# Hybrid encoder layer: a fourth product pair in the gate-up stage, weight sums by an accumulating transfer, and eight gated tiles kept in HBM

## The chip, the core and the metric

The kernel runs on one core of a Trainium2 chip. The metric is the device time of one execution in microseconds (us). The core has a TensorE (PE) for matrix products, a VectorE (DVE), a ScalarE (ACT), a GpSimd (POOL) and a SyncE (SP), which work at the same time and wait for each other through semaphores. Each takes its own instructions strictly in the order in which they stand. Sixteen DMA engines move data between HBM and the on-chip memory (SBUF). SP issues nearly all transfers here, through a queue that is served in hardware; GpSimd can issue transfers too, and it prepares their descriptors in software. TensorE accumulates into the banks of PSUM.

## What is computed

One encoder layer on 256 tokens of width 2048, in float32: a feed-forward block (FFN), a mixing block, and a second FFN, each with a norm before and after it. The change touches the two FFNs alone.

```python
D_MODEL, SEQ, D_FF = 2048, 256, 5632

def rms_norm(x, gain):
    return x * lax.rsqrt(jnp.mean(x * x, axis=-1, keepdims=True) + EPS) * gain

def swiglu(x, w_gate_up, w_down):              # w_gate_up: 2048 x 11264, w_down: 5632 x 2048
    gate, up = jnp.split(x @ w_gate_up, 2, axis=-1)
    return (jax.nn.silu(gate) * up) @ w_down

x = x + 0.5 * rms_norm(swiglu(rms_norm(x, pre1), w1_gate_up, w1_down), post1)
h = rms_norm(x, pre_m); p = h @ W_in
x = x + rms_norm(concat(hgrn2(p), attention(p)) @ W_out, post_m)
x = x + 0.5 * rms_norm(swiglu(rms_norm(x, pre2), w2_gate_up, w2_down), post2)
```

## The kernel before, in words

**A product in three.** A float32 value is split into a high part `h` (a copy by ScalarE that rounds to the type TensorE multiplies, L176) and a low part `l` (the rest, a subtraction on VectorE, L177). A product of two such values is three matmuls: high by high, high by low, low by high (`three`, L435; the matmul is L441). Nearly all of TensorE's time is L441.

**The gate-up stage** of an FFN (`ffn`, L894) runs over 11 groups `g` (0 to 10) of 512 gate columns and 512 up columns. In each group it goes through eight pairs `u` (0 to 7): a pair is two blocks of 128 rows of the weights, 256 rows by 1024 columns, 1 MB, loaded by two transfers of 512 KB into a tile `raw` (L152; a pool `rawp` of three such tiles). The columns of `raw` are four blocks of 512: `b11`, `b12` (first 128 rows, gate and up), `b21`, `b22`. The split of a pair goes in halves of 1024 columns into tiles of two pools of five (`hip` for `h`, `lop` for `l`), so ScalarE and VectorE can be at most five halves ahead of TensorE.

**Plain and mixed pairs.** A plain pair is 8 products, 24 matmuls, from two split halves. A mixed pair (`seven`, L463) takes one of Winograd's forms of Strassen's scheme: it sees the pair as a 2x2 matrix of blocks and uses seven products, 21 matmuls, of sums of blocks. The sums of the activations are made once per FFN (`sums_in`, L934, kept as tiles `xs`). The sums of the weights are made each time, in place in `raw`:

```python
split_act(h, l, b11)                                         # one block of 512
four[:, 0:2] = four[:, 0::3] + four[:, 1:2]                  # L473: b11 + b12, b22 + b12
lower = split_half(raw, 1)                                   # b21, b22
b22 = b11 + b22                                              # L477
upper = split_half(raw, 0)
b21 = b22 + b21                                              # L479
last = split_half(raw, 1)
```

So a mixed pair costs three matmuls less than a plain one, and on VectorE an L473, an L477, an L479, a half block of 512 and a third half of 1024 more. The pairs 2, 4 and 6 are mixed from group 2 on, 2 and 4 in group 1, none in group 0. The four partial sums of the seven products are folded into the group's banks (`fold`, L507) near the end of a group: eight additions on VectorE (L516 to L539).

**After a group** `units` (L954) applies silu and the product of gate and up (L959, L960), turns the result on TensorE (L971, eight transposes) and splits it into two tiles `ht` of 512 KB, 22 in all, which are the left sides of the down stage. They lie in two pools, `late` (8) and `early` (14), until the down stage has used them.

**The down stage** (`Pairs`, L586) runs twice over the 22 pairs of the down weights (1024 output columns each), plain and mixed pairs in turn, in an order that is written out by hand (`orders`, L1009). It uses the same `raw`, `hip` and `lop`.

**Order.** The places of the instructions on each engine come from a scheduler that works before the run, with its own estimates; only a few stretches are fixed by hand. On the chip the order on each engine, SP and POOL among them, is fixed, and a late instruction holds back all that stand behind it.

## Time and profile before

| | |
|---|---|
| median of 3 runs | 1836.19 us (1835.5 to 1836.25) |
| span of the profiled execution | 1835.7 us |
| PE busy | 1821.5 us, 99% |
| DVE busy | 1620.7 us, 88% |
| ACT busy | 1099.7 us, 60% |
| POOL busy | 23.3 us, 1% |
| moved by DMA | 365.77 MB, 199 GB/s on the mean |
| POOL's own transfers | 0.14 MB |

The profile gives no time of the profiled execution beside its span, and the span lies within the three runs. A line such as L441 is one of the kernel before. "Busy" is the time in which an engine worked on something; a matmul's end is modelled, so the pace of TensorE is read from the distance between the starts of its matmuls, not from their durations. In a timeline a row is a start, a duration, the engine, the line, the operation and a count of equal instructions, with the idle time before the first of them and what ended it in brackets. A table of windows gives, for each stretch of the span, the busy time of each engine, the clock that was granted to TensorE, the busy share of the 16 DMA engines, and the rate in GB/s.

### The profile page before, as it was taken

The numbers are of one execution on the slowest core, as the hardware profiler recorded it, in microseconds if no ns is written. First come the engines' busy times: TensorE is split into PE (matmuls) and PEld (weight loads), VectorE is DVE, ScalarE is ACT, GpSimd is POOL, SyncE is SP. The second block draws the span as 40 slices with busy tenths as digits, with TensorE's granted clock in tenths as the row PEclk, the third lists the DMA queues.
The fourth block names the chain that finished last, engine by engine and source line by source line (L and its number), as shares of the span: only waits on it lengthen the run. The fifth ranks groups of instructions, "written<-read, shape, count | busy, mean of one in ns | idle before, by whom it ended". The sixth has DMA issues, their size and how long they took to land.

```text
span 1835.7 us, 22980 instructions
## 1 busy us (share of the span) xinstructions
PE 1821.5 (99%) x8492; PEld 1516.5 (83%) x8492; DVE 1620.7 (88%) x2047; ACT 1099.7 (60%) x1454; POOL 23.3 (1%) x39
## 2 busy tenths in 40 slices
PE   9999999999999999999999999999999999999998
PEld 7888888888888888888888888888888888888786
DVE  7989999999999998477787798989999999999897
ACT  7555555555666567476587556455556555566563
POOL 1000000000000001000000000000000000000000
PEclk9999999999999999999999999999999999999999
DMA  7555555556555576555454456555555555545564
GB/s 255 206 178 213 207 200 191 184 188 215 205 208 216 195 260 212 199 182 174 163 170 150 167 210 224 190 195 190 213 193 192 213 212 195 205 187 206 201 229 177
DMA packets 174737, 365.77 MB, mean 199 GB/s; under 512 B 9256, under 2 KB 44160, under 8 KB 173856
## 3 DMA queue, kind: packets, MB, share of 16 engines
q1 hardware_dynamic: 174272, 364.17, 56.0%
q8 instruction: 66, 1.08, 0.2%
q14 instruction: 47, 0.39, 0.1%
q0 software_dynamic: 352, 0.14, 0.0%
HBM read 360.06 MB, written 4.21 MB: 198 GB/s over the span
## 4 chain that ended last, share of the span: by engine, by line
PE 94%; ACT 2%; DVE 2%; DMA 1%; issue 0%; POOL 0%; DVEq 0%; SPq 0%; ACTq 0%; POOLq 0%
PE pa L441 40%; PE pb L441 36%; PE pa L309 5%; PE pa L314 3%; PE pa L364 2%; PE pa L362 2%; PE pa L363 2%; DMA raw<-in_w_ffn_down_dram 1%; DVE l L177 1%; ACT h L176 1%; PE pb L971 1%; PE pa L971 1%; PE pb L1376 0%; PE pb L1350 0%; PE pb L1454 0%
## 5 line engine op out<-in xcount | busy, mean ns | idle before, releaser
L176 ACT CAST h<-raw 128x1024 fp32r<-128x1024 f32 (+1 forms) x825 | 821.5, 1021 | 538.2 <-PE pb L441 146.9
L177 DVE TENSOR_TENSOR l<-raw,h 128x1024 fp32r<-128x1024 f32 (+1 forms) x825 | 950.1, 1180 | 135.7 <-ACT h L176 106.0
L441 PE MATMUL pa<-h,xt 128*128 128x512 f32 x1176 | 409.5, 390 | 0.1
L441 PE MATMUL pb<-h,xt 128*128 128x512 f32 x1060 | 376.9, 392 | 0.0
L441 PEld LDWEIGHTS pa<-h,xt 128*128 128x128 f32 x1176 | 220.8, 188 | 46.1 <-DVE xt L232 0.6
L441 PEld LDWEIGHTS pb<-h,xt 128*128 128x128 f32 x1060 | 199.0, 188 | 41.6 <-DVE pb L537 0.6
L441 PE MATMUL pa<-l,xt 128*128 128x512 f32 x588 | 229.2, 390 | 0.0
L441 PE MATMUL pb<-l,xt 128*128 128x512 f32 x530 | 206.4, 389 | 0.0
L441 PE MATMUL pb<-h,ht 128*128 128x512 f32 x464 | 163.5, 390 | 0.0
L441 PE MATMUL pa<-h,ht 128*128 128x512 f32 x464 | 162.7, 389 | 0.0
L441 PEld LDWEIGHTS pa<-l,xt 128*128 128x128 f32 x588 | 110.4, 188 | 23.4 <-DVE l L177 0.8
L473 DVE TENSOR_TENSOR raw<-raw 128x1024 f32<-128x1024 f32 x102 | 124.3, 1219 | 1.1
L309 PE MATMUL pa<-xt,h 128*128 128x512 f32 x512 | 124.4, 393 | 0.2 <-ACT h L176 0.2
L441 PEld LDWEIGHTS pb<-l,xt 128*128 128x128 f32 x530 | 99.6, 188 | 19.6
L309 PEld LDWEIGHTS pa<-xt,h 128*128 128x128 f32 x512 | 93.8, 188 | 18.6 <-ACT h L176 0.6
L441 PEld LDWEIGHTS pa<-h,ht 128*128 128x128 f32 x464 | 87.1, 188 | 18.1
L441 PEld LDWEIGHTS pb<-h,ht 128*128 128x128 f32 x464 | 87.1, 188 | 18.0
L441 PE MATMUL pb<-l,ht 128*128 128x512 f32 x232 | 90.3, 389 | 0.0
L441 PE MATMUL pa<-l,ht 128*128 128x512 f32 x232 | 90.3, 389 | 0.0
L441 PE MATMUL pa<-h,xs 128*128 128x512 f32 x232 | 80.8, 389 | 0.0
L441 PE MATMUL pb<-h,xs 128*128 128x512 f32 x232 | 80.8, 389 | 0.0
L479 DVE TENSOR_TENSOR raw<-raw 128x512 f32<-128x512 f32 x102 | 70.1, 688 | 1.8
(281 smaller groups left out, 2360.6 us busy)
## 6 DMA issues: line engine op xcount, KB each, us to landing
raw<-in_w_ffn_gate_up_dram SPq DMA_DIRECT2D x350, 512.0 KB, 4.7
raw<-in_w_ffn_down_dram SPq DMA_DIRECT2D x88, 1024.0 KB, 5.0
raw<-in_w_mix_in_dram SPq DMA_DIRECT2D x52, 1024.0 KB, 4.9
raw<-in_w_mix_out_dram SPq DMA_DIRECT2D x16, 1024.0 KB, 4.9
pg<-in_post_norm_ffn_dram SPq DMA_DIRECT2D x4, 512.0 KB, 7.4
X<-in_x_dram SPq DMA_DIRECT2D x2, 1024.0 KB, 8.4
bias<-row SPq DMA_DIRECT2D x16, 128.0 KB, 5.0
kept<-X SPq DMA_DIRECT2D x2, 1024.0 KB, 4.1
```

Of the source, the lines that this page charges most:

```text
L176: nc.scalar.copy(hi, src)
L177: nc.vector.tensor_tensor(lo, src, hi.bitcast(F32), ALU.subtract)
L309: nc.tensor.matmul(slot[f], weights(hs, kk, f), xcol(xt, k), start=(k == 0), stop=(k == KT - 1))
L314: nc.tensor.matmul(slot[f][:, 0:T], weights(ls, kk, f), xcol(xt, kh * 8 + kk, 0), start=False, stop=False,)
L362: nc.tensor.matmul(dst, xh, h[:, o : o + n], start=(k == 0), stop=False)
L363: nc.tensor.matmul(dst, xh, l[:, o : o + n], start=False, stop=False)
L364: nc.tensor.matmul(dst, xl, h[:, o : o + n], start=False, stop=(k == KT - 1))
L441: nc.tensor.matmul(self.bank(at), lhs, rhs, start=(n == 1), stop=n in (ends, self.of[at]), skip_group_check=n > ends,)
L473: nc.vector.tensor_tensor(four[:, 0:2], four[:, 0::3], four[:, 1:2].to_broadcast([P, 2, 512]), ALU.add)
L479: nc.vector.tensor_tensor(b21, b22, b21, ALU.add)
L971: nc.tensor.transpose(bank[:, o : o + P], zs[m][:, k * P : (k + 1) * P], ident)
```

## The change

In both FFNs the pairs 2, 3, 4 and 6 are mixed from group 2 on, and 2 and 3 in group 1. L473 is no longer done by VectorE: after each pair, `prepare` loads the mixed pair that is the third from there (two pairs lie between), splits its `b11` into tiles of their own (`h1`, `l1`, three each), and then has GpSimd read `b12` and `b22` from HBM once more and add them to `b11` and `b12` in SBUF during the transfer. The `raw` tiles of the pairs 2, 3 and 6 come from a new pool of two (`gated.room`), that of pair 4 from `rawp`. The room for that is made by keeping the first eight `ht` tiles in HBM: they are stored in the groups 1 to 4, two after pair 4 of each, and fetched again at the start of the down stage into the place of the new pool. The first order of the down stage is changed so that those eight come after seven others.

```diff
-    def load(src, between=None):
-        raw = rawp.tile([P, 2048], F32, tag="raw", name=nm("raw"))
+    def load(src, between=None, pool=rawp, **kw):
+        raw = pool.tile([P, 2048], F32, tag="raw", name=nm("raw"), **kw)
...
         def seven(self, u, aside=None):
 
-            raw = load(self.source(u))
+            ready = self.prepared.pop(u, None)
+            raw = ready[0] if ready else load(self.source(u))
...
-            h, l = self.one_block()
-            split_act(h, l, b11)
-
-            nc.vector.tensor_tensor(
-                four[:, 0:2], four[:, 0::3], four[:, 1:2].to_broadcast([P, 2, 512]), ALU.add
-            )
+            if ready:
+                h, l = ready[1:]
+            else:
+                h, l = self.one_block()
+                split_act(h, l, b11)
+
+                nc.vector.tensor_tensor(
+                    four[:, 0:2], four[:, 0::3], four[:, 1:2].to_broadcast([P, 2, 512]), ALU.add
+                )
             lower = split_half(raw, 1)
...
-    MIXED_IN = (2, 4, 6)
+    MIXED_IN = (2, 3, 4, 6)
+    LEAD = 3
+    AWAY = 8
...
+        def prepare(self):
+
+            at, g = self.pos + LEAD - 1, self.g
+            if at >= KT // 2:
+                at, g = at - KT // 2, g + 1
+            if g >= NG or (at not in self.mixed if g == self.g else at not in self.sums):
+                return
+            src = self.source(at, g)
+            raw = load(src, pool=rawp if at == MIXED_IN[2] else self.room, bufs=3 if at == MIXED_IN[2] else 2)
+            h, l = (self.room.tile([P, 512], F32R, tag=t, name=nm(t), bufs=3) for t in ("h1", "l1"))
+            split_act(h, l, raw[:, 0:512])
+            nc.gpsimd.dma_start(
+                raw[:, 0:1024].rearrange("p (k c) -> p k c", k=2), src[:, :, 1], accum_op=ALU.add
+            )
+            self.prepared[at] = raw, h, l
...
-            early_cm = tc.tile_pool(name=nm("he"), bufs=NU - LATE, reuse_waits="tile")
+            early_cm = tc.tile_pool(name=nm("he"), bufs=NU - LATE - AWAY, reuse_waits="tile")
             early = early_cm.__enter__()
-            hts, sums = [], {}
+            room_cm = tc.tile_pool(name=nm("gx"), bufs=1, reuse_waits="tile")
+            gated.room = room_cm.__enter__()
+            hts, sums, away = [], {}, {}
...
+            def put_away(u):
+                away[u] = dram.tile([P, 1024], F32, tag=f"ht{u}", name=nm("away"))
+                nc.sync.dma_start(away[u], hts[u].bitcast(F32).rearrange("p k i t -> p (k i t)"))
+
+            def fetch(u):
+                hts[u] = back.tile([P, 2, 2, T], F32R, tag="ht", name=nm("ht"))
+                nc.sync.dma_start(hts[u].bitcast(F32).rearrange("p k i t -> p (k i t)"), away[u])
...
-                    pool = early if g < NU - LATE else late
+                    pool = early if AWAY <= g < NU - LATE else late
...
-                    if g == 1 and u == 5:
-                        sums_in(MIXED_IN[2])
+                    if g == 1 and u in (5, 6):
+                        sums_in(MIXED_IN[u - 3])
+                    if u == 4 and 0 < g <= AWAY // 2:
+                        put_away(2 * g - 2)
+                        put_away(2 * g - 1)
+                    gated.prepare()
                 waiting = units(gated.c, rest if g else rs2)
                 next(waiting)
+            room_cm.__exit__(None, None, None)
             close_far()
+            back_cm = tc.tile_pool(name=nm("hb"), bufs=AWAY, reuse_waits="tile")
+            back = back_cm.__enter__()
             orders = [
-                [1, 3, 0, 5, 2, 7, 4, 9, 6, 11, 8, 13, 10, 15, 12, 14, 17, 16, 19, 18, 20, 21],
+                [9, 11, 8, 13, 10, 15, 12, 1, 14, 3, 0, 5, 2, 7, 4, 6, 17, 16, 19, 18, 20, 21],
...
             rows.work(2, lambda: next(waiting))
+            for i, u in enumerate((1, 3, 0, 5, 2, 7, 4, 6)):
+                fetch(u)
+                rows.work(3 + i // 2)
```

More of the change, by code (lines that the diff above doesn't have):

```diff
@@ L411, in __init__ @@
             self.tiles, self.sums = tiles, sums
+            self.prepared = {}
         def begin(self, order, c=None):
@@ L860, in group, with source @@
             self.begin(range(KT // 2), c)
-        def source(self, u):
-            return self.w[:, 2 * u : 2 * u + 2, :, self.g * 512 : (self.g + 1) * 512]
+        def source(self, u, g=None):
+            g = self.g if g is None else g
+            return self.w[:, 2 * u : 2 * u + 2, :, g * 512 : (g + 1) * 512]
         def left_sums(self, u):
             return self.sums[u]
+        def prepare(self):
[12 more added lines that the diff above has]
+            self.prepared[at] = raw, h, l
         def see(self, xt):
@@ L938, in sums_in @@
                 ws = sums_of(whole, room_for("s").rearrange("p (j t) -> p j t", j=4))
-                w = work.tile([P, 4, 2, P], F32R, tag="sp", name=nm("xs"), bufs=3)
+                apart = u == MIXED_IN[1]
+                w = (gated.room if apart else work).tile(
+                    [P, 4, 2, P], F32R, tag="sp", name=nm("xs"), bufs=1 if apart else 3
+                )
                 split_act(w[:, :, 0, :], w[:, :, 1, :], ws)
                 gated.sums[u] = w
+            def put_away(u):
[4 more added lines that the diff above has]
+                nc.sync.dma_start(hts[u].bitcast(F32).rearrange("p k i t -> p (k i t)"), away[u])
             def folded():
@@ L1024, in ffn @@
             rows.work(NU - 4)
+            back_cm.__exit__(None, None, None)
             early_cm.__exit__(None, None, None)
```

## The prediction, written before the changed kernel ran

> **What bounds the kernel now.** I read the page first (busy shares, the chain of waits), then the chain in order of time through the gate-up stage, then windows of one gate-up group each, then VectorE's timeline and waits within one group, then single transfers.
>
> ```profile
> span 1835.7 us, 22980 instructions
> PE 94%; ACT 2%; DVE 2%; DMA 1%; issue 0%; POOL 0%; DVEq 0%; SPq 0%; ACTq 0%; POOLq 0%
> 112.22 2.72 PE pa L441 x12
> 154.60 2.72 PE pa L441 x12
> 196.97 2.72 PE pa L441 x12
> 154.60:196.97 42.37, 42.37 (x192) 35.19 (x192) 39.41 (x47) 24.42 (x28) 0.00 (x0) 1.00 0.56 199
> 196.97:239.34 42.37, 42.37 (x193) 35.18 (x192) 39.41 (x47) 24.42 (x28) 0.00 (x0) 1.00 0.56 199
> 234.89 0.27 PE L971 MATMUL pa<-ident,z 128*128 128x128 f32 x1
> 235.00 0.27 PE L971 MATMUL pa<-ident,s 128*128 128x128 f32 x1
> ```
>
> The chain is TensorE. The same place of the gate-up loop returns every 42.37 us, and a run of 12 matmuls takes 2.72, so 0.2267 each; a group with three mixed and five plain pairs has 3x21 + 5x24 = 183 of them, 41.48 us, and eight transposes at 0.11 (from start to start) make 42.36. TensorE has no idle time there, at full clock. But the same windows show VectorE busy for 39.41 of 42.37. Its waits in the second window:
>
> ```profile
> DVE l L177 <- ACT h L176: 2.4, 2, 1.2
> DVE ht L177 <- ACT ht L176: 0.2, 1, 0.2
> 198.22 5.23 DVE L177 TENSOR_TENSOR l<-raw,h 128x1024 fp32r<-128x1024 f32 x5 [1.17 <-ACT h L176]
> 203.37 1.22 DVE L473 TENSOR_TENSOR raw<-raw 128x1024 f32<-128x1024 f32 x1
> 204.62 0.69 DVE L477 TENSOR_TENSOR raw<-raw 128x512 f32<-128x512 f32 x1
> 205.35 0.69 DVE L479 TENSOR_TENSOR raw<-raw 128x512 f32<-128x512 f32 x1
> 205.96 5.37 DVE L177 TENSOR_TENSOR l<-raw,h 128x1024 fp32r<-128x1024 f32 x5
> 217.53 4.63 DVE L177 TENSOR_TENSOR l<-raw,h 128x1024 fp32r<-128x1024 f32 x4 [1.19 <-ACT h L176]
> 224.42 1.21 DVE L177 TENSOR_TENSOR l<-raw,h 128x1024 fp32r<-128x1024 f32 x1
> 225.55 0.68 DVE L516 TENSOR_TENSOR z<-pb,s 128x512 f32<-128x512 f32 x1
> ```
>
> VectorE's idle time of a group is two waits of 1.17 and 1.19: after L479 it must wait until ScalarE has copied the half just summed (1.05) before it can subtract. That is a dependency inside VectorE's own work, not a wait for TensorE. So work, 42.37 - 2.6 = 39.8, and these waits fill the period: **VectorE is a second chain as long as TensorE's**, and a shorter TensorE alone buys little.
>
> **What the change takes from TensorE.** Nine groups of each FFN (2 to 10) get a fourth mixed pair: three matmuls of 0.2267 less, 18 x 0.68 = 12.2 us in all, 41.68 a group. The built program has 54 matmuls less, and GpSimd has 76 new transfers, 38 per FFN, so the change does what it says.
>
> **VectorE's work per group.** Away go three L473 of 1.25 at most (203.37 to 204.62): -3.6 at 1.2. The fourth mixed pair adds an L177 of 1024 columns (1.13, from 224.42 to 225.55) and an L177 of 512, an L477 and an L479 (0.61 to 0.73 from start to start; 2.0 together). 39.8 - 3.6 + 1.1 + 2.0 = 39.3. The waits after L479 become 1.2 at pair 6, and 0.5 at pairs 3 and 4, where the built order puts an `l1` of 0.6 in between; at pair 2 small work fills it: 2.2. Sum 41.5, just under TensorE's 41.68.
>
> **The new loads.** The two tiles of the new pool hold three pairs in turn (2, 3, 6, 2, ...), and a load waits for the last subtraction of the pair two places before. VectorE's built order around two of these, in the middle of the stage (tile 468 is pair 2, 482 pair 3, 514 pair 6, 495 pair 4, 541 pair 2 of the next group):
>
> ```
> L177 TensorTensor l_503_2574<-raw_468_2438,h_502_2573 128x1024
> L177 TensorTensor l_509_2603<-raw_482_2491,h_508_2602 128x1024
> L177 TensorTensor l_511_2608<-raw_482_2491,h_510_2607 128x1024
> L482 TensorTensor raw_482_2491<-raw_482_2491 128x512
> L484 TensorTensor raw_482_2491<-raw_482_2491 128x512
> L177 TensorTensor l1_516_2641<-raw_514_2637,h1_515_2640 128x512
> L177 TensorTensor l_513_2613<-raw_482_2491,h_512_2612 128x1024
> L177 TensorTensor l_518_2646<-raw_495_2555,h_517_2645 128x1024
> L177 TensorTensor l_520_2651<-raw_495_2555,h_519_2650 128x1024
> L482 TensorTensor raw_495_2555<-raw_495_2555 128x512
> L484 TensorTensor raw_495_2555<-raw_495_2555 128x512
> L177 TensorTensor l1_543_2800<-raw_541_2796,h1_542_2799 128x512
> ```
>
> The first row frees tile 514, and VectorE has four instructions, 2x1.13 + 0.65 + 0.72 = 3.6 us, until it needs its first block; the seventh row frees 541, again with 3.6 to go. What such a load takes:
>
> ```profile
> L152 SPq DMA_DIRECT2D raw<-in_w_ffn_gate_up_dram x1: 540/540/540, 218.8 to 218.8; - x1
> DMA to landing us min/median/max: 3.7/3.7/3.7
> 222.57 1.05 ACT L176 CAST h<-raw 128x1024 fp32r<-128x1024 f32 x1 [0.67 <-DMA raw<-in_w_ffn_gate_up_dram]
> L176 ACT CAST h<-raw 128x512 fp32r<-128x512 f32 x60 | 37.2, 619 | 0.8
> raw<-in_w_ffn_gate_up_dram SPq DMA_DIRECT2D x350, 512.0 KB, 4.7
> raw<-in_w_ffn_gate_up_dram SPq DMA_DIRECT2D x10, 512.0 KB, 7.6
> 10.00:15.00 5.00, 5.00 (x27) 4.10 (x27) 4.26 (x6) 3.92 (x9) 0.00 (x0) 1.00 1.04 398
> ```
>
> A lone load goes from its issue at 218.8 to ScalarE's start at 222.57, 3.8 us; with the copy of 512 columns, 0.62, and the steps between, VectorE's `l1` can start 4.5 us after the release. It waits 0.9, twice a group. Behind the waiting `h1` on ScalarE stands the last copy of the pair before, behind the waiting `l1` its subtraction, and TensorE waits for both. (For pair 3 the order leaves 5.9 us; no wait.) The load of the next pair 2 also meets the accumulating transfer of pair 6, which starts with it. The 7.6 is the median while the engines were full (the last row: 1.04 of them, 398 GB/s), 3.7 alone; 512 KB at 398 GB/s are 1.3 us. That wait is 0.9 to 2.2; I take 1.6, the middle. A group: 41.5 + 0.9 + 1.6 = 44.0, **1.6 more than before**.
>
> One rule bears on the middle taken here. The Trainium skill, "DMA: Bandwidth & Descriptors", section "Issuing engines are not separate DMA queues", says that transfers issued by SP, ACT and GpSimd run on the same 16 engines and interleave. By it the load pays the full 2.2, and the sum below would be 10 higher; GpSimd's few transfers of 4 KB at the start took 5.3 us to land and its 16 KB one later 1.8, which agrees.
>
> **Groups that differ.** In groups 2, 3 and 4 the order leaves 5.8, 4.7 and 4.7 us for pair 6 and 3.6, 4.3, 4.3 for the next pair 2, but two stores of 512 KB stand in SP's queue directly ahead of pair 6's load: 1 MB at 398 GB/s is 2.6 us, half of it before the load is issued, +1.3. Waits 0 + 1.6, 1.1 + 0.9, 1.1 + 0.9: 0.7, 1.1 and 1.1 over 42.37. Groups 5 to 9: 5 x 1.6 = 8.2. Group 10 has no next pair 2: 42.4, nothing. Per FFN 11.1, **both 22**. In group 1 two L473 go (-2.4) and one `sums_in` comes, five instructions of at most 0.7: within 1, taken as 0.
>
> **The accumulating transfer** itself has no row. From below it is a lone load, 3.7; from above a load (4.7) and a store (4.1 for 1 MB) one after the other, 8.8; GpSimd's own issue adds 0.5 for 16 and for 32 rows, so I take 1 for 256, and 6 to 7 in all. The shortest distance between an `l1` and the first use of its sums is pair 6's, 9.9 us of VectorE's work plus the waits above, less ScalarE's copy of 1.05: hidden up to about 10. If it isn't, ScalarE's copy of the upper half waits, and all behind it.
>
> ```profile
> kept<-X SPq DMA_DIRECT2D x2, 1024.0 KB, 4.1
> 4.21 0.53 POOL L115 DMA_DIRECT2D rows<-in_pre_norm_mix_dram  x1 [1.79 <-PE pb L119]
> 23.54 0.54 POOL L1123 DMA_DIRECT2D bias_rows<-in_onehot_dram  x1 [15.84 <-DMA raw<-in_w_ffn_gate_up_dram]
> rows<-in_hgrn_out_norm_dram POOLq DMA_DIRECT2D x1, 4.0 KB, 5.3
> row<-bias_rows POOLq DMA_DIRECT2D x1, 16.0 KB, 1.8
> 500.00:520.00 20.00, 20.00 (x90) 16.58 (x89) 20.00 (x27) 12.32 (x14) 0.00 (x0) 1.00 0.63 230
> 582.66 8.09 DMA raw<-in_w_ffn_down_dram
> 600.00:620.00 20.00, 19.49 (x86) 15.83 (x85) 18.44 (x21) 11.31 (x13) 0.00 (x0) 1.00 0.47 182
> 1720.00:1740.00 20.00, 18.72 (x82) 14.85 (x81) 18.50 (x19) 11.03 (x12) 0.00 (x0) 1.00 0.54 210
> ```
>
> **The down stage and the lead.** VectorE and ScalarE may be five halves ahead of TensorE, 5 x 2.72 us at most, and such a lead could swallow a part of the 11. But before, the down stage uses it up: VectorE is full there (20.00 of 20), and TensorE loses 0.5 us around 605 and 1.3 around 1730, where the chain passes through a load of 8.09. What VectorE loses in the gate-up stage comes out there at the latest. The fetches add 4.2 MB, 10.5 us at 398 GB/s, among the first loads of the run, with nothing of their own needed before the eighth pair: 0 to 6 per FFN, taken as 1.5, since the engines are 0.63 busy there and loads already late. **+3.** The new order itself keeps the pattern of plain and mixed pairs, and counts as nothing.
>
> **Sum.** 1835.7 + 22 + 3 = 1860.7; the median of the runs is 0.5 above that span: **1861 us**.
>
> **The rivals.** *VectorE keeps up (chance 0.24).* The waits of 0.9 fall where VectorE would have stood anyway, and TensorE sets the pace: 1836.2 - 12.2 = 1824. For it: without the load waits VectorE's sum is 41.5 against 41.68; 0.5 us less in VectorE's work or in the loads decides half of it. Against it: both terms of the wait are measured and no gap in VectorE's rows is longer than its own waits. This is the other side; it decides if a load reaches VectorE in 3.6 us rather than 4.5. *The transfer or the engines are too slow (0.13).* A group moves 8.39 MB at 0.56 of the engines; four accumulations of 0.52 MB at one, two, three and four times the cost of a plain byte make it 0.70, 0.84, 0.98 and 1.12. At four times a group takes 1.12 x 42.37 - 0.5 = 47, +4.6, and 18 of them +83: 1919. For it: an accumulation reads two places and writes one. Against it: that is two, not four. *It balances (0.08).* The waits shrink by a good half: within 0.2% of 1836.
>
> **How the numbers follow.** The likeliest, VectorE as the pace, has 0.55; its own range is 1842 (waits of 0.9 alone, 11 less; fetches at 0; VectorE's work 0.3 lower, 5 less) to 1880 (2.2 at the second load, 10 more; fetches at 6, 9 more). The range given reaches to the first rival and into the second: 1822 to 1898. Something like 0.2%, 3.7 us, is what a measurement of this kernel can tell from no change. Faster 0.24, within that 0.08, slower 0.55 + 0.13 = 0.68.
>
> **What would show it.** In the profile after: 4x21 + 4x24 = 180 matmuls in a gate-up group, a period near 44.0 with TensorE idle 2 us of it, released by L177; VectorE waiting for ScalarE's `h1`, and `h1` for the load of `raw`, about 1 us at pair 6 and 1 to 2 at pair 2; groups 2 and 10 the shortest. Wrong if the period is 41.7; if `h` of the upper half waits for GpSimd's transfer (then it is slower than 10 us); if the loads are late because the engines' share is over 0.9; or if the time is lost in the down stage.

## The result, and the profile after

The changed kernel takes 1905.04 us (median of four runs, 1900.37 to 1909.02) against 1836.22 for the kernel before beside it: 1.0375 times as long, interval 1.0353 to 1.0396. Slower was forecast, at 1861 and at most 1898; the loss is 69 us where 25 was expected. The granted clock of TensorE was 0.989, 0.987, 0.984 and 0.983 in the four runs, in the order of their times. The profiled execution is the shortest of them (1900.37 us), and the comparisons of traces below are between profiled executions.

The page of the changed kernel: span, busy times, the DMA queues, the chain that ended last (by engine, then by line), and two rows of the DMA issues (count, KB each, median us to landing). L442, L478, L482 and L484 are the L441, L473, L477 and L479 of before.

```profile
span 1898.3 us, 23223 instructions
PE 1835.0 (97%) x8438; PEld 1513.2 (80%) x8438; DVE 1611.9 (85%) x2071; ACT 1113.7 (59%) x1492; POOL 115.5 (6%) x115
q1 hardware_dynamic: 178880, 380.95, 57.2%
q0 software_dynamic: 21024, 39.99, 13.0%
PE 60%; DVE 18%; DMA 11%; ACT 6%; issue 4%; POOL 0%; ACTq 0%; SPq 0%; DVEq 0%; POOLq 0%
PE pa L442 23%; PE pb L442 21%; DVE l L177 10%; DMA raw<-in_w_ffn_gate_up_dram 9%; PE pa L309 5%; ACT h L176 4%; DMA raw<-in_w_ffn_down_dram 3%; PE pa L314 3%; PE pa L364 2%; PE pa L362 2%; PE pa L363 2%; DVE raw L478 1%; DVE raw L484 1%; D
raw<-in_w_ffn_gate_up_dram POOLq DMA_DIRECT2D x76, 512.0 KB, 6.0
ht<-away SPq DMA_DIRECT2D x16, 512.0 KB, 7.0
```

The chain was TensorE for 94% of the span; now it is TensorE for 60%, and the rest runs through loads of the weights, ScalarE's copies and VectorE's subtractions. TensorE has 54 matmuls fewer (8492 to 8438), as it should, yet is busy for longer: some of its matmuls run at a lower clock, as the windows below show.

Where the 62.6 us between the two spans arise, by the starts of the transposes that end each group (L971 before, L1008 after):

| stretch | before | after | difference |
|---|---|---|---|
| start to the transposes of group 0 | 64.5 | 72.3 | +7.8 |
| ten groups, first FFN | 424.6 | 451.1 | +26.5 |
| down stage, mixing block, second FFN's group 0 | 691.8 | 692.3 | +0.5 |
| ten groups, second FFN | 424.6 | 451.8 | +27.2 |
| second down stage to the end | 230.2 | 230.8 | +0.6 |

The groups 5 to 9 take 47.0 us on the mean (45.3 to 49.4) against 42.4 before; group 2 takes 45.7 and 44.8, the groups 3 and 4 between 42.6 and 43.1, group 10 takes 42.5 and 42.6. Three groups in the table of windows (start:end, then length, busy time of PE, PEld, DVE, ACT and POOL with counts, PEclk, share of the DMA engines, GB/s):

```profile
341.20:388.20 47.00, 43.94 (x190) 35.70 (x189) 39.24 (x48) 25.45 (x30) 6.11 (x5) 0.96 0.80 228
388.20:433.70 45.50, 42.23 (x189) 34.53 (x188) 38.91 (x48) 25.25 (x30) 4.37 (x4) 1.00 0.77 225
433.70:480.90 47.20, 44.09 (x190) 35.69 (x189) 37.99 (x44) 25.02 (x29) 5.40 (x5) 0.96 0.81 229
```

TensorE is idle for 3 us in each, VectorE for 6.6 to 9.2, the DMA engines are busy for 0.8 instead of 0.56, and in two of the three the granted clock falls to 0.96. VectorE's waits in the last of these groups, from its timeline (start, duration, engine, line, operation, count, and in brackets the idle time before and what ended it):

```profile
438.04 3.49 DVE L177 TENSOR_TENSOR l<-raw,h 128x1024 fp32r<-128x1024 f32 x3 [1.17 <-ACT h L176]
444.18 0.69 DVE L177 TENSOR_TENSOR l<-raw,h 128x512 fp32r<-128x512 f32 x1 [1.32 <-ACT h L176]
453.17 0.69 DVE L177 TENSOR_TENSOR l<-raw,h 128x512 fp32r<-128x512 f32 x1 [3.21 <-ACT h L176]
462.40 3.50 DVE L177 TENSOR_TENSOR l<-raw,h 128x1024 fp32r<-128x1024 f32 x3 [1.19 <-ACT h L176]
```

And ScalarE's row that releases the longest of them:

```profile
452.52 5.35 ACT L176 CAST h<-raw 128x512 fp32r<-128x512 f32 x6 [5.52 <-DMA raw<-in_w_ffn_gate_up_dram]
```

The two rows of 512 columns are the `l1` of pair 6 and of the next pair 2. They are the waits that the prediction named: 1.32 where it had 0.9, and 3.21 where it had 1.6 and at most 2.2. Over the whole run VectorE waits 62.4 us at its `l1`, and ScalarE 170.4 at its `h1`, by the groups of instructions with the forms kept apart:

```profile
L177 DVE TENSOR_TENSOR l<-raw,h 128x512 fp32r<-128x512 f32 x78 | 53.4, 686 | 62.4 <-ACT h L176 62.4
L176 ACT CAST h<-raw 128x512 fp32r<-128x512 f32 x78 | 48.4, 622 | 170.4 <-DMA raw<-in_w_ffn_gate_up_dram 151.7 <-PE pb L442 14.8 <-PE pa L442 3.8
```

The start is another matter. GpSimd's timeline in the changed kernel:

```profile
34.70 1.28 POOL L887 DMA_DIRECT2D raw<-in_w_ffn_gate_up_dram  x1 [9.08 <-DVE l L177]
40.91 1.22 POOL L887 DMA_DIRECT2D raw<-in_w_ffn_gate_up_dram  x1 [4.92 <-issue]
41.69 1.06 POOL L186 TENSOR_TENSOR r<-v,mhalf 128x1 f32<-128x1 f32 x1
```

`r` is the last step of the norm ahead of the FFN, and the scaled activations wait for it. Its input `v` is there at 36.3, but on GpSimd it stands behind two accumulating transfers, and the second of these is issued only when the first has landed (34.70 + 6.0 = 40.7). TensorE stands still for most of five us and then starts at a low clock:

```profile
40.00:45.00 5.00, 0.41 (x2) 0.42 (x3) 1.49 (x9) 1.04 (x1) 2.39 (x3) 0.71 0.97 264
45.00:50.00 5.00, 5.00 (x17) 4.09 (x17) 4.97 (x6) 0.00 (x0) 0.00 (x0) 0.61 0.74 210
```

### The profile page after: what moved, and what is told of

It reads as the page before. It is cut to its first block, busy times and chain, and to the rows that moved or that the text cites. A ratio compares the mean times of both kernels' runs of the same rounds, so it can differ in the third digit from the quotient of the medians.

```text
span 1898.3 us, 23223 instructions
## 1 busy us (share of the span) xinstructions
PE 1835.0 (97%) x8438; PEld 1513.2 (80%) x8438; DVE 1611.9 (85%) x2071; ACT 1113.7 (59%) x1492; POOL 115.5 (6%) x115
## 3 DMA queue, kind: packets, MB, share of 16 engines
q0 software_dynamic: 21024, 39.99, 13.0%
## 4 chain that ended last, share of the span: by engine, by line
PE 60%; DVE 18%; DMA 11%; ACT 6%; issue 4%; POOL 0%; ACTq 0%; SPq 0%; DVEq 0%; POOLq 0%
PE pa L442 23%; PE pb L442 21%; DVE l L177 10%; DMA raw<-in_w_ffn_gate_up_dram 9%; PE pa L309 5%; ACT h L176 4%; DMA raw<-in_w_ffn_down_dram 3%; PE pa L314 3%; PE pa L364 2%; PE pa L362 2%; PE pa L363 2%; DVE raw L478 1%; DVE raw L484 1%; DVE raw L482 1%; DVE ht L177 1%
## 5 line engine op out<-in xcount | busy, mean ns | idle before, releaser
L176 ACT CAST h<-raw 128x1024 fp32r<-128x1024 f32 (+1 forms) x861 | 836.0, 1012 | 569.2 <-DMA raw<-in_w_ffn_gate_up_dram 162.0
L177 DVE TENSOR_TENSOR l<-raw,h 128x1024 fp32r<-128x1024 f32 (+1 forms) x861 | 983.3, 1170 | 204.0 <-ACT h L176 176.3
L442 PE MATMUL pa<-h,xt 128*128 128x512 f32 x1104 | 391.7, 396 | 4.3 <-DVE s L525 3.1
L442 PE MATMUL pb<-h,xt 128*128 128x512 f32 x952 | 345.1, 395 | 0.3 <-DVE z L521 0.3
L442 PEld LDWEIGHTS pa<-h,xt 128*128 128x128 f32 x1104 | 211.1, 191 | 52.3 <-DVE s L525 5.0
L442 PE MATMUL pa<-l,xt 128*128 128x512 f32 x552 | 218.2, 395 | 0.5 <-DVE l L177 0.5
L442 PEld LDWEIGHTS pb<-h,xt 128*128 128x128 f32 x952 | 180.9, 190 | 38.4 <-DVE z L521 0.8
L442 PE MATMUL pb<-l,xt 128*128 128x512 f32 x476 | 187.2, 393 | 0.0
L442 PE MATMUL pb<-h,ht 128*128 128x512 f32 x464 | 163.5, 390 | 0.0
L442 PE MATMUL pa<-h,ht 128*128 128x512 f32 x464 | 163.1, 389 | 0.0
L887 POOL DMA_DIRECT2D raw<-in_w_ffn_gate_up_dram x76 | 92.7, 1220 | 814.8 <-DVE l L177 589.2
L442 PE MATMUL pb<-h,xs 128*128 128x512 f32 x304 | 111.1, 399 | 28.4 <-ACT h L176 28.3
L442 PEld LDWEIGHTS pa<-l,xt 128*128 128x128 f32 x552 | 105.7, 191 | 23.5 <-DVE l L177 1.4
L442 PE MATMUL pa<-h,xs 128*128 128x512 f32 x304 | 105.9, 389 | 0.0
L442 PEld LDWEIGHTS pb<-l,xt 128*128 128x128 f32 x476 | 90.6, 190 | 18.1
L442 PEld LDWEIGHTS pa<-h,ht 128*128 128x128 f32 x464 | 87.1, 188 | 18.2
L442 PEld LDWEIGHTS pb<-h,ht 128*128 128x128 f32 x464 | 87.1, 188 | 18.0
L442 PEld LDWEIGHTS pb<-h,xs 128*128 128x128 f32 x304 | 57.7, 190 | 44.9 <-ACT h L176 34.4
L442 PE MATMUL pa<-l,ht 128*128 128x512 f32 x232 | 90.4, 390 | 0.0
L442 PE MATMUL pb<-l,ht 128*128 128x512 f32 x232 | 90.3, 389 | 0.0
```

Of the source, the lines that this page charges most:

```text
L176: nc.scalar.copy(hi, src)
L177: nc.vector.tensor_tensor(lo, src, hi.bitcast(F32), ALU.subtract)
L442: nc.tensor.matmul(self.bank(at), lhs, rhs, start=(n == 1), stop=n in (ends, self.of[at]), skip_group_check=n > ends,)
L887: nc.gpsimd.dma_start(raw[:, 0:1024].rearrange("p (k c) -> p k c", k=2), src[:, :, 1], accum_op=ALU.add)
```

## The experiments

Three theories of the gate-up stage went into the runs. Theory 1: a place in SBUF comes free too late. Theory 2: the transfers themselves are the cost. Theory 3: VectorE's work alone sets the pace. Times are medians; a time without an interval is a single run.

**The transfers left out.**

```diff
             split_act(h, l, raw[:, 0:512])
-            nc.gpsimd.dma_start(
-                raw[:, 0:1024].rearrange("p (k c) -> p k c", k=2), src[:, :, 1], accum_op=ALU.add
-            )
```

> Leaves out the sums b11 + b12 and b22 + b12 of the prepared mixed pairs (GpSimd's accumulating transfers are gone, nothing is put in their place; VectorE, ScalarE, TensorE and SP do what they did). Theory 1 (a place in SBUF comes free too late: the load of h1's block can only be issued when the pair two places before is done, and h1 and l1 stand in the engines' order ahead of work that is ready): the load of the next pair 2 still lands 4.0 to 4.8 us after its issue, VectorE still waits 0.9 to 1.5 for it, the groups 5 to 9 take 43.5 to 45 us (46 to 47 with the transfers, 42.4 before), and the run ends at 1850 to 1875. Theory 2 (the transfers themselves are the cost: they make the loads beside them late, and the upper halves wait for them): the groups take 41.7 to 42.5, ScalarE's wait for raw falls to the 20 us in all of before, and the run ends at 1825 to 1840. Theory 3 (VectorE's work alone sets the pace): no change, 46 to 47 and 1895 or more. In each theory the start of the run gives back the 7.8 us that GpSimd's r lost behind the first two transfers, if that is what it stood behind.

1845.46 us. The groups 5 to 9 take 42.7 to 43.5, and the first transposes come at 66.1. The transfers are most of the cost: without them the kernel takes 7 us more than the kernel before, with them 63 (by the spans, 1843.1 and 1898.3). But it is not all of it: the run lies between the ranges of theories 1 and 2, and two load waits are still there, at the size that the prediction had worked out. A group of this kernel, VectorE's timeline and the window:

```profile
375.42 0.69 DVE L177 TENSOR_TENSOR l<-raw,h 128x512 fp32r<-128x512 f32 x1 [0.90 <-ACT h L176]
382.13 0.69 DVE L177 TENSOR_TENSOR l<-raw,h 128x512 fp32r<-128x512 f32 x1 [0.93 <-ACT h L176]
365.90:408.80 42.90, 42.14 (x190) 34.54 (x189) 38.95 (x48) 25.25 (x30) 0.00 (x0) 1.00 0.57 197
L177 DVE TENSOR_TENSOR l<-raw,h 128x512 fp32r<-128x512 f32 x78 | 53.5, 687 | 24.2 <-ACT h L176 24.2
```

So 0.93 becomes 3.21 by the transfers, and 24.2 us in the run become 62.4. The load that stands behind the 0.93 and the one behind the 3.21, each as a row of its issues with the landing under it; first without the transfers:

```profile
L152 SPq DMA_DIRECT2D raw<-in_w_ffn_gate_up_dram x2: 540/576/612, 377.6 to 378.2; - x2
DMA to landing us min/median/max: 3.8/4.6/5.4
```

then in the changed kernel, together with GpSimd's transfer issued before it:

```profile
L887 POOL DMA_DIRECT2D raw<-in_w_ffn_gate_up_dram x1: 1219/1219/1219, 445.3 to 445.3; - x1
DMA to landing us min/median/max: 5.8/5.8/5.8
...
L152 SPq DMA_DIRECT2D raw<-in_w_ffn_gate_up_dram x2: 539/592/646, 446.4 to 447.0; - x2
DMA to landing us min/median/max: 6.1/6.4/6.8
```

The first of the two loads carries `b11`; it lands 3.8 us after its issue, and 6.1 where GpSimd's transfer was issued 1.1 us ahead of it. The difference of 2.3 is that of VectorE's waits (3.21 - 0.93). Two windows of the changed kernel, columns as before, show what the engines do meanwhile:

```profile
447.40:450.00 2.60, 2.60 (x13) 2.12 (x13) 2.52 (x4) 0.00 (x0) 0.00 (x0) 1.00 1.00 163
450.60:452.60 2.00, 0.64 (x3) 0.19 (x1) 0.00 (x0) 0.08 (x1) 0.00 (x0) 1.00 1.05 406
```

In the first the engines are full with GpSimd's transfer alone, at 163 GB/s; in the second they are full with the loads, at 406. By the packets of the trace, GpSimd's transfer moves from 447.2 to 450.8, and the load that was issued at 446.4 begins at 450.2, 3.8 us after its issue; without the transfers it begins 1.3 us after (377.6, then 379.0). So the load stands behind nearly the whole transfer.

**Places earlier.** Each of the pairs 2, 3 and 6 has its own tile; ten gated tiles lie in HBM, and the first order of the down stage takes the other places first.

```diff
-    AWAY = 8
+    AWAY = 10
...
-            raw = load(src, pool=rawp if at == MIXED_IN[2] else self.room, bufs=3 if at == MIXED_IN[2] else 2)
+            raw = load(src, pool=rawp if at == MIXED_IN[2] else self.room, bufs=3)
...
-                [9, 11, 8, 13, 10, 15, 12, 1, 14, 3, 0, 5, 2, 7, 4, 6, 17, 16, 19, 18, 20, 21],
+                [11, 13, 10, 15, 12, 1, 14, 3, 0, 5, 2, 7, 4, 9, 6, 8, 17, 16, 19, 18, 20, 21],
```

> The pairs 2, 3 and 6 have a raw tile each (three in the pool in place of two), paid for by two more gated tiles kept in HBM (ten in place of eight); the transfers stay. A load is then issued a whole group ahead of the use of the block before in its place. Theory 1 (places come free too late): ScalarE's and VectorE's waits for raw in the gate-up stage go (from 162 us in all to below 60), the groups 5 to 9 take 41.7 to 43, the gate-up stages give back 40 to 55 us, and the run ends at 1845 to 1865 (the 7.8 of the start stay). Theory 2 (the transfers make loads late, or the DMA engines are full): loads still land after 6 to 7 us and the engines' share stays 0.8, the groups stay at 45 or more, 1885 or more. Theory 3 (VectorE's work sets the pace): no change of the groups, 1900.

1885.23 us (1.0256, 1.0236 to 1.0277). The groups 5 to 9 take 43.8 to 45.4, between the two theories: of the 4.6 us that such a group lost the places give back 2.5 (47.0 to 44.5 on the mean), the rest stays. ScalarE's waits for raw fall from 162.0 to 116.0 us, not below 60. In the chain of waits of one group, the load in the middle was issued when its place came free:

```profile
414.03 1.23 DVE l L177
415.26 0.02 issue
415.28 6.04 DMA raw<-in_w_ffn_gate_up_dram
421.31 0.02 issue
421.34 0.63 ACT h L176
```

It is the load of pair 4, whose place comes from `rawp`, and it too takes 6 us. The same edit without the transfers:

> Three tiles for the pairs 2, 3 and 6, and the accumulating transfers left out (with them the sums b11 + b12 and b22 + b12). Theory 1 and 2 together (late places cost 0.9 us a load; the transfers make the loads late; both matter): with the places early and the engines free the groups come to TensorE's 41.7 to 42.1, and the run ends at 1822 to 1832. Rival (VectorE's work with its own waits is the bound, 41.5 plus what the order loses): the groups stay at 42.4 to 43 and the run at 1836 to 1845.

1847.49 us, as good as with the short places (1845.46), and 2 us above both ranges that were expected. This does not show that late places are free without the transfers. The load of pair 4 is still late, so VectorE's waits at its `l1` only fall from 24.2 to 21.0 us in the run (from 1.9 to 1.3 in a group of 5 to 9), and in the order that was built with the third tile its waits at the halves of 1024 columns grow instead (from 1.95 to 2.70 in a group). What late places cost by themselves stays open.

**What is missing to TensorE's own pace.** With no transfers and a tile for each of the pairs 2, 3 and 6, the groups 2 to 9 still took 42.2 to 43.9. The same kernel with one VectorE addition of the prepared pairs left out:

```diff
-            nc.vector.tensor_tensor(b22, b11, b22, ALU.add)
+            if not ready:
+                nc.vector.tensor_tensor(b22, b11, b22, ALU.add)
```

> Three tiles for the pairs 2, 3 and 6, no transfers, and in the prepared pairs the addition L482 is left out as well (leaves out three of the four weight sums of those pairs): VectorE does 4 x 0.69 = 2.75 us less in a group, all else as in the kernel with early places and no transfers, whose groups took 42.2 to 43.9. If VectorE with its waits is what holds that kernel above TensorE's 41.7: the groups take 41.7 to 42, and the run ends at 1822 to 1832. Rival (the loads, or TensorE's own waits for ScalarE): the groups stay at 42.5 to 43.5, 1840 or more.

1827.8 us, and each of the groups 2 to 10 of both FFNs takes 41.7. The table of windows shows TensorE without a gap:

```profile
240.00:480.00 240.00, 240.00 (x1081) 199.25 (x1080) 207.70 (x242) 148.34 (x171) 0.00 (x0) 1.00 0.58 204
```

So VectorE is the second bound, as the prediction had it: 2.75 us less of its work in a group take the groups 5 to 9 from 43.0 on the mean to TensorE's own 41.7, and the saving on TensorE is the 0.7 a group that was worked out.

**Engine time, or the presence of a transfer.** Two kernels halve the cost of the transfer in different ways: one copies the same bytes without adding, one adds half the bytes.

```diff
-                raw[:, 0:1024].rearrange("p (k c) -> p k c", k=2), src[:, :, 1], accum_op=ALU.add
+                raw[:, 0:1024].rearrange("p (k c) -> p k c", k=2), src[:, :, 1]
```

> GpSimd's transfer of b12 and b22 stays where it was, with the same bytes, place and issue, but it copies in place of adding (leaves out the two weight sums: b11 and b12 are overwritten by b12 and b22). Theory A (what costs is the time of the 16 engines, which an accumulated byte takes about twice: share 0.82 with the transfers, 0.56 without): the share of a group falls to 0.68 to 0.71, the groups 5 to 9 take 43 to 44.5 us (42.8 without the transfers, 46 to 47 with them), and the run ends at 1855 to 1875. Theory B (what costs is that there is a transfer at all between l1 and the upper half, and GpSimd's queue): landing stays 5 us or more, groups 45 to 47, 1885 or more.

```diff
-            nc.gpsimd.dma_start(
-                raw[:, 0:1024].rearrange("p (k c) -> p k c", k=2), src[:, :, 1], accum_op=ALU.add
-            )
+            nc.gpsimd.dma_start(raw[:, 0:512], src[:, 0, 1], accum_op=ALU.add)
```

> The accumulating transfer brings b12 alone, half the bytes (leaves out the sum b22 + b12). If the loss goes with the engines' time it is half of that of the whole transfer: 1843 + 30 = 1873, between 1860 and 1885, at a share of 0.69. If it sits in the number of transfers (their issue, their completion): 1890 or more. If it is the crowding that comes only above a share of 0.8: below 1855. At the start, the second transfer was issued when the first had landed, 6.2 us after it: if GpSimd's place for descriptors holds one transfer of this size, two of half the size are issued one behind the other, 1 to 3 us apart; if it always waits for the landing, 4 us or more.

1877.83 and 1875.72 us. GpSimd's queue (packets, MB, share of the 16 engines), first of the copy, then of the half sum:

```profile
q0 software_dynamic: 11296, 39.99, 6.3%
```

```profile
q0 software_dynamic: 11296, 20.06, 6.6%
```

Twice the bytes by copy take the engines' time of the bytes added, packet for packet, and both kernels end within 2 us of each other. The whole transfer has 21024 packets and 13.0%: 0.130 x 1898.3 / 76 = 3.2 us of all 16 engines each, against 1.6 for the copy (0.063 x 1875.8 / 76). So the loss follows the engines' time rather than the bytes, since the two kernels agree, but not in proportion: with half of it two thirds of the loss are there (1875 between 1843 and 1892, the spans with none and with all, the start taken out), and the groups 5 to 9 take 46.0 and 45.7 on the mean. The expectation of 43 to 44.5 for the copy missed that, and its 1875 by 3; its groups lie in the range of theory B, so a part of the cost that does not shrink with the engines' time is not ruled out.

**GpSimd's order at the start.**

```diff
-        nc.gpsimd.tensor_tensor(r, v, mhalf[:, 0:1], ALU.pow)
+        last["r"] = nc.gpsimd.tensor_tensor(r, v, mhalf[:, 0:1], ALU.pow)
...
+            with tc.issue_after(last["r"].ins):
                 nc.gpsimd.dma_start(
```

> Only GpSimd's order: r of the norm ahead of the FFN (the power at the end of rsqrt_of) stands ahead of the accumulating transfers. Theory of the start: r was 7 us late since it stood behind two transfers, the second of which was issued only when the first had landed; r starts within 1 us of v, the first mark comes at 64 to 66 us in place of 72.3, and the run is 6 to 8 us shorter, 1897 to 1899. Rival (the start is late since the new loads of the first groups take the DMA engines): r is early, but the first mark stays at 70 or later and the run above 1903.

1893.21 us (1.0300, 1.0279 to 1.0320). `r` starts at 36.30, the first transposes at 66.5 instead of 72.3: the theory of the start holds for 5.8 of the 7.8 us. The other 2.0 (64.5 before) were not followed up. The half transfer and the copy had the same cure by other means. In the kernel with the half sum GpSimd issues two, one behind the other, and `r` follows at 36.55:

```profile
34.87 1.82 POOL L887 DMA_DIRECT2D raw<-in_w_ffn_gate_up_dram  x2 [9.59 <-DVE l L177]
36.55 0.76 POOL L186 TENSOR_TENSOR r<-v,mhalf 128x1 f32<-128x1 f32 x1
```

So GpSimd issued two transfers of half the packets at once, where the second whole one had waited for the first to land. What holds it back there was not looked into.

**Both edits, and a place for each mixed pair.**

> Both of the edits before: three tiles for the pairs 2, 3 and 6, and r ahead of the transfers. If both theories hold, they add up: 1838 to 1858; with the groups at TensorE's own pace of 41.7 it is 1825 to 1838, below the kernel before. If the DMA engines bound it, 1878 or more.

1882.35 us (1.0241, 1.0224 to 1.0258), where 1838 to 1858 was expected if the two edits added up: the groups take 43.5 to 45.3 as with the places alone, and the first transposes come only at 73.7 (76.1 with the places alone, 66.5 with `r` alone), so the early places cost something at the start. With a fourth tile (twelve gated tiles in HBM, an order to match):

```diff
-    AWAY = 8
+    AWAY = 12
...
-            raw = load(src, pool=rawp if at == MIXED_IN[2] else self.room, bufs=3 if at == MIXED_IN[2] else 2)
+            raw = load(src, pool=self.room, bufs=4)
...
-                [9, 11, 8, 13, 10, 15, 12, 1, 14, 3, 0, 5, 2, 7, 4, 6, 17, 16, 19, 18, 20, 21],
+                [13, 15, 12, 17, 14, 1, 0, 3, 2, 5, 4, 7, 6, 9, 8, 11, 10, 16, 19, 18, 20, 21],
```

> A raw tile each for all four mixed pairs (twelve gated tiles kept in HBM, and an order of the down stage that goes with it), r ahead of the transfers. In the kernel with three tiles the one wait left before the folding is that for pair 4's load, whose place came free 5.3 us before. Theory 1: that wait goes and the groups take 42 to 43.5 in place of 44.5, 1845 to 1865. Theory 2 (at a share of 0.82 every load is late, the plain pairs' too): 44 or more, 1870 or more, with the down stage a little longer for four more stores and fetches.

1866.55 us (1.0154, 1.0125 to 1.0184), 1.5 above the range of theory 1, whose groups these are: with the transfers unchanged, at a share of 0.83 of the engines, the groups 5 to 9 take 41.7 to 45.6, 43.2 on the mean against 46.9 with `r` first alone, and VectorE's wait at its `l1` is back at 24.2 us. So a transfer costs little where no load that queues behind it is urgent. The start lost 10 us (76.8 against 66.5): ScalarE waited up to 12.7 for a load in the first group. Why that load came late in this kernel was not followed up.

**The transfers without the fourth pair.** The pairs 2, 4 and 6 of before, their sums by transfer, r first.

```diff
-    MIXED_IN = (2, 3, 4, 6)
+    MIXED_IN = (2, 4, 6)
```

> The pairs 2, 4 and 6 alone are mixed, as in the kernel before, but their sums come by the accumulating transfer, and r stands ahead of the transfers: the transfers without the fourth pair. VectorE has 3 x 1.2 = 3.6 us less to do in a group than before, TensorE the same 42.4. Theory (late loads cost only where VectorE is the bound, for then nothing makes up for a wait): the groups take 42.4 to 42.9, and the run ends at 1837 to 1848. Rival (loads that are made late stop TensorE whatever VectorE has in reserve): 44 us or more in the groups 5 to 9, 1865 or more.

1857.55 us (1.0111, 1.0081 to 1.0140), between the two. The groups 5 to 9 take 43.0 on the mean (42.4 to 44.1), 0.6 above before. Two things can hide the transfers there, and this run does not separate them: VectorE has a reserve, and with three mixed pairs the pool of two gives pair 2 and pair 4 a tile each, so their places come free early. The groups 1 to 4 take 44.6 in the first FFN, and in the groups 2 and 3 ScalarE waits for loads five times, 16.0 us in all; there the reserve does not help.

**VectorE makes the sums again**, at the place of before, with the loads and `b11`'s split as early as in the changed kernel.

> Four mixed pairs, prepared as in the changed kernel, but VectorE makes the sums again (L473's addition of 1.2 us at its old place), no accumulating transfers: what the fourth pair costs without them. VectorE's 42.8 of the kernel without the sums + 4 x 1.2 = 47.6, some of it in places where VectorE waited for a load of 0.9: 46 to 47.6 in the groups 5 to 9, and the run ends at 1895 to 1925, no better than with the transfers. Rival (the sums hide in VectorE's waits): 44 to 45, 1860 to 1885, and then the transfers cost more than the additions that they save.

1925.05 us; the groups 5 to 9 take 46.1 to 50.1. Here the four pairs cost more by VectorE than by the transfers.

**GpSimd adds, from SBUF.** The transfer is replaced by an addition at its place.

```diff
+            with tc.issue_after(last["r"].ins):
+                nc.gpsimd.tensor_tensor(
+                    four[:, 0:2], four[:, 0::3], four[:, 1:2].to_broadcast([P, 2, 512]), ALU.add
+                )
```

> The sums b11 + b12 and b22 + b12 of the prepared pairs by an addition on GpSimd (128x1024, from SBUF) at the place of the transfer, r ahead of them. The one addition of this kind in the trace took GpSimd 1.26 us for 128x512, so 2.5 each and 10 in a group. Theory A (the engines' traffic is the cost): as without the transfers, groups of 42.8, share 0.56, the run at 1840 to 1850. Theory B (the sums at this place and their semaphores are the cost): groups of 45 or more, 1880 or more. Rival C (GpSimd and VectorE hinder each other when both add in SBUF): VectorE's l of 128x1024 takes longer than 1.17 us while GpSimd adds; 4 x 2.5 us of that at half speed is 5 us a group, 1900.

1993.94 us (1.0861, 1.0840 to 1.0883): rival C, and by more than was feared. The groups 5 to 9 take 50.2 to 52.0. GpSimd's additions are as long as expected, but VectorE's subtractions beside them are not. GpSimd's and VectorE's timelines:

```profile
381.28 2.39 POOL L889 TENSOR_TENSOR raw<-raw 128x1024 f32<-128x1024 f32 x1 [12.95 <-DVE l L177]
381.41 5.61 DVE L177 TENSOR_TENSOR l<-raw,h 128x1024 fp32r<-128x1024 f32 x3 [0.26 <-ACT h L176]
410.18 2.40 POOL L889 TENSOR_TENSOR raw<-raw 128x1024 f32<-128x1024 f32 x1 [17.19 <-DVE l L177]
410.57 3.09 DVE L177 TENSOR_TENSOR l<-raw,h 128x1024 fp32r<-128x1024 f32 x1
```

Three subtractions take 5.61 us instead of 3.50, one takes 3.09 instead of 1.22: VectorE all but stands still while GpSimd adds (1.9 of the 2.0 us in which the single one overlaps with the addition). This test could therefore not tell theory A from B. Three more of the same kind show the same: with early places, with b22 = b11 + b22 on GpSimd too, and that with the short places.

> The same with three tiles for the pairs 2, 3 and 6. Theory A: groups of 42.2 to 43.5 as in the kernel with early places and no transfers, 1840 to 1850 (the places are not what is missing). Theory B: 44 or more. Rival C: as above.

> And L482 (b22 = b11 + b22) of the prepared pairs on GpSimd too: VectorE has 2.75 us less in a group, GpSimd 4 x 1.26 more. If VectorE is what holds the groups above TensorE's 41.7, as e10 has it: 41.7 to 42.2, the run at 1824 to 1834, below the kernel before by 0.1 to 0.6%. If the upper block now waits for GpSimd (l of the lower half, 1.26 us, L484, then the copy of the last half): 43 or more, 1845 or more. Rival C: more.

> The same with the places of the changed kernel (two tiles for three pairs). The two load waits of 0.9 us are back; VectorE's 2.75 us pay for them: groups of 41.7 to 42.4, 1826 to 1838. If the waits for late places cannot be made up: 42.8, 1845.

1950.39 us (1.0624, 1.0603 to 1.0645), 1992.53 (1.0859, 1.0840 to 1.0877) and 2034.40 (1.1082, 1.1059 to 1.1104). None of the kernels that compute the whole layer beats the kernel before.

## Why the prediction was wrong

**What held.** The saving: 54 matmuls, and 41.7 us a group where nothing else holds TensorE (the run that leaves out L482). VectorE as the second chain: 2.75 us less of its work bring the group from 42.2 to 43.9 down to 41.7. The two waits for late places: 0.9 each by the working, 0.90 and 0.93 measured without the transfers. Their sum with VectorE's work was a little high: 41.5 + 1.8 = 43.3 for such a group, 43.0 measured on the mean. Group 10 (nothing) and group 1 came as forecast, and the accumulating transfer lands in 6.0 us with 1.22 of issue (6 to 7 and 1 taken) and is hidden: of the 162.0 us that ScalarE's copies wait for raw, 151.7 are at those of 512 columns, and the upper half is not one of these. The down stages cost 1.1 us (3 taken).

**The step that failed is one term of the sum:** "The load of the next pair 2 also meets the accumulating transfer of pair 6, which starts with it. [...] That wait is 0.9 to 2.2; I take 1.6, the middle." It is 3.2 in the group shown, 3.5 on the mean of the groups 5 to 9, and above 2.2 in every one of them. The upper bound added 1.3 us, the time of 512 KB as a plain load at the engines' full rate. The transfer takes all engines for 3.2 us, twice a copy's, and is issued 1.1 us ahead of the load, so 0.9 + 3.2 - 1.1 = 3.0 would have been an estimate, next to the 3.2 measured; that close it comes by luck, since the transfer's packets start only 1.9 us after its issue. The text had the doubling at hand: its second rival argued that an accumulation counts for two, and used it for the engines' capacity (0.84 forecast, 0.80 measured, under 1) but not for the load that queues behind it. A share under 1 says that the engines keep up on the mean, not that an urgent load does.

**What followed from it** was not in the sum at all: the clock. A group of 5 to 9 loses 4.6 us against before, not 1.6. Its length can be taken apart. In the groups in which the clock stays whole, it is 41.1 us plus VectorE's waits at its `l1`, in the changed kernel and in the four that keep its places and its VectorE work (means over those of the ten groups, waits summed from VectorE's timelines):

| kernel | groups at whole clock | length | waits at `l1` | difference |
|---|---|---|---|---|
| transfers left out | 10 | 42.96 | 1.88 | 41.08 |
| half the sum | 5 | 44.54 | 3.48 | 41.06 |
| copy | 4 | 44.53 | 3.46 | 41.07 |
| `r` first | 1 | 44.91 | 3.85 | 41.06 |
| changed kernel | 3 | 45.56 | 4.48 | 41.08 |

So the form of the sum was right, with 41.1 in place of 41.5: a group is longer by just what these waits add. The other seven groups of the changed kernel take 1.5 to 1.6 us more than 41.1 and their waits, one of them 2.3 more, and in each of the seven the granted clock is at half for 3.41 us (6.83 in the one). Three windows around the half clock of the first group shown above:

```profile
359.55:362.96 3.41, 1.29 (x4) 0.86 (x5) 2.76 (x3) 3.41 (x5) 1.22 (x1) 1.00 0.12 42
362.96:366.37 3.41, 3.41 (x9) 2.65 (x8) 3.41 (x4) 1.69 (x2) 0.00 (x0) 0.50 1.03 176
366.37:369.78 3.41, 3.41 (x16) 2.81 (x15) 2.18 (x4) 1.69 (x2) 0.00 (x0) 1.00 1.05 405
```

Nine matmuls fall into the second window and 16 into the third. TensorE had stood idle for 2.31 us up to 360.91, where the late load of pair 2 holds up ScalarE's next copy. Of the 4.0 us on the mean above the kernel without transfers, then, 2.5 are the wait at pair 2 (3.47 against 0.94), 0.3 that at pair 6 (1.27 against 0.95), and 1.2 the clock. With a tile for each of the pairs 2, 3 and 6 the longest idle time of TensorE in these groups is 1.75 us and the clock stays whole in all ten: 1.2 of the 2.5 us that those places gave back are the clock. Over the whole run the granted clock is 0.999 before and without the transfers, 0.989 with them, 0.996 with early places.

The Trainium skill, "TensorE: Matmul & The Clock Gate", Part 1, has the clock at half after an idle window of about 3.4 us that runs freely. The stretch of 3.41 us agrees, and so does it that one group lost the clock after 2.31 us of idle time and the group before it, with 2.31 as well, did not. But the idle time was shorter than such a window, and in the 3.41 us ahead of the half clock TensorE was busy for 1.29: it did not take a wholly idle window here.

**By groups.** The pattern was right (5 to 9 most, 10 nothing), but group 2 lost 3.3 and 2.4 us instead of 0.7, for the same reason as 5 to 9, and the stores ahead of pair 6's load, priced at 1.3, cost little: the groups 3 and 4 lose 0.2 to 0.7 in all instead of 1.1.

**The start** was taken as nothing: group 1 was worked through, group 0 was not. It cost 7.8 us, 5.8 of them because `r` is GpSimd's too. The prediction priced GpSimd's issue at 1 us; it did not ask what stands behind the second issue when the first has not landed.

**The rivals.** "The transfer or the engines are too slow" (1919) came nearest in time, and by the right kind of cause, but at twice the price of a plain byte rather than four times: the engines were not full, they were in the way. "VectorE keeps up" (1824) is what the run without L482 reaches (1827.8): it needed 2.75 us less of VectorE's work, no transfers and a tile for each of the pairs 2, 3 and 6, not the half us that was named.

## What to carry to other kernels

A transfer that moves work off a busy engine is paid where an urgent load queues behind it: price it by the time it takes the DMA engines (here 3.2 us for 512 KB accumulated, 1.6 copied), laid on the nearest load whose place comes free late, and not by the mean share of the engines. The place matters as much as the transfer: with `r` first, the groups 5 to 9 took 46.9 us with three pairs in two tiles and 43.2 with a tile for each mixed pair, and 43.0 with the late places and no transfers. A wait that lets TensorE stand idle for 2.3 us can cost again by the clock, here 1.6 us a time. When work is put on an engine that was idle, list what that engine already does, and what stands behind the new work.

## What the runs showed of the hardware

- An accumulating transfer of 512 KB by GpSimd went in packets half as long as the copy of the same bytes (21024 against 11296 packets in all), at nearly the same time of the engines per packet (0.19 and 0.17 us, their share times 16 spans over the packets), so twice per byte. While it ran alone the engines were full at 163 GB/s, with plain loads at 406.
- GpSimd issued the second whole transfer only when the first had landed (34.70, then 40.91), but two with half the packets in 1.8 us.
- A GpSimd addition of 128x1024 stopped VectorE's subtraction for 1.9 of the 2.0 us in which they overlapped (1.22 became 3.09). The Trainium skill, "GPSIMD Engine Reference", section 8, "Key points", says that the two engines share their SBUF interfaces and contend when a VectorE instruction has two inputs in SBUF, as this one has; the trace agrees and gives the size. The copy and the accumulating transfer, issued by the same engine, left VectorE's 1.22 as it was.
- The granted clock went to half for 3.41 us, once for 6.83, after TensorE had been idle for 2.3 to 4.1 us at a time in a group of the changed kernel, but not every time after 2.3 to 2.9 us; in the kernel with the half sum 1.5 us were enough once. In the changed kernel 3.41 us at half clock cost a group 1.5 to 1.6 us.
